# Blocks of expert slots in a two-layer decoder trunk: 14 for 16, with experts ranked by token count on chip

## Chip, cores, metric

One core of a Trainium2 chip. The metric is device time in microseconds (us) of one execution of the whole program: two layers, one launch.

## What is computed

Each of two layers has a mixer (attention over dilated windows and a convolution), a mixture of experts, and a gated input per layer. The change is in the mixture of experts. The reference, cut to that part (512 tokens, width 1024, 32 experts in 4 groups of 8, expert width 512, float32):

```python
gsel = argmax(h @ w_rg + b_rg)                 # one group per token
top_v, top_i = top_k(le[gsel], 2)              # two experts of that group, le = h @ w_re + b_re
gate = softmax(lg)[gsel] * softmax(top_v)
eid = gsel * 8 + top_i
...
hb = silu(xb @ w_gate[e]) * (xb @ w_up[e])     # xb: the tokens of expert e
out[tok] += gate * (hb @ w_down[e])
```

512 tokens choose two experts each, so 32 experts share 1024 rows. All 32 experts' weights are needed in each layer: 3 matrices of 2 MB each, as 12 tiles of 128x1024 float32 (512 KB) per expert, 384 tiles per layer.

## The kernel before

**Slots and blocks.** Every expert has `CAP` = 64 slots; a token's slot number is 64 times its expert plus its rank among that expert's tokens. Two experts make a block of 128 slots (a "pair", `p`), two blocks make a chunk `c`; a layer has 16 blocks in 8 chunks. An expert with more than 64 tokens is served by a loop (`overflow`, line 1213), whose number of rounds is computed on chip and read into registers.

**One chunk.** `onehots` builds, on VectorE, the 0/1 matrices that pick the chunk's 256 slots; `gather` turns them into the slots' activations (ps_xg, 64 matmuls of two terms, high and low); `gate_up` runs the gate and the up product of each block (ps_g, ps_u), with the 64 slots of an expert as the stationary operand and the weight tile streaming; the two experts of a block write the two halves of the same PSUM tile. `hidden` forms silu times up, `transp` turns it (ps_hT), `down` is the third product (ps_y), and `combine` adds the rows back to the tokens with the transposed 0/1 matrix (ps_c). The order on TensorE is written out in `moe`'s loop over `c`: gate and up of chunk c, down of chunk c-1, transposes of chunk c, gather for chunk c+1, combine of chunk c-1. After the combine of `c == OVC` (4) comes the loop for crowded experts; at `c` = 4 the table of the per-layer input is loaded (`load_embeddings`), and at 5 and 6 it is multiplied.

**Weights.** `pump` (line 234) issues the tiles from SP in the order of `self.items`: gate and up of two blocks, then down of the two before. A tile takes a buffer of pool `s4`, shared with everything else of the layer, and may be loaded as soon as a buffer is free; `KEEP` holds some back in each chunk. Before the expert stage, during the mixer, `RING` = 6, 18, 28 limits how many weight tiles may already be there at three points; another 8 half tiles (`late_items`, line 246) go to the other pool. All these loads go through SP's one queue, in program order: a load that waits for its buffer holds up all behind it. Each also waits for the landing of the one eight before.

**Routing.** For each of the four token tiles, `count` and `slots` find a token's experts and its slot (line 889 on); `route` then counts the tokens of each expert, and works out gates and the loop's rounds. The matmuls whose order is fixed are recorded through a wrapper class, so they all stand under line 94.

Of the kernel before, what the change touches and what calls it, by code (L numbers as in the profile page):

```python
# [26 lines left out]
CAP = 64  # L27
GS = 256
NPAIR = NE // 2
# [3 lines left out]
C_N1 = 592  # L33
# [23 lines left out]
RING = 6, 18, 28  # L57
KEEP = 6, 10, 6, 6, 8, 10, 12, 8
LAGS = 1, 2, 1, 5
OVC = 4  # L60
# [95 lines left out]
class Trunk:  # L156
    def __init__(self, ctx, tc, x, pT, wd, wg, wu, wdn, sm, gains, cst, out):
# [18 lines left out]
        self.items, self.item_tile, self.item_next, self.ring = [], {}, 0, 0  # L176
# [610 lines left out]
    def route_init(self):  # L787
# [3 lines left out]
        self.spos, self.base, self.slots = ([self.tn(4, f"{n}{i}") for i in range(2)] for n in ("sp", "sb", "sl"))  # L791
# [5 lines left out]
    def route_tile(self, t):  # L797
# [93 lines left out]
        pe.matmul(po, self.trib, mb(t), start=t == 0, stop=True)  # L891
        for i in range(2):
# [10 lines left out]

    def route(self):

        nc = self.nc
        v, act, pe = nc.vector, nc.scalar, nc.tensor
        for t in range(NT):
            pe.matmul(self.posb[:, 128:160], self.oneb, self.Mb[:, t * 32:(t + 1) * 32], start=t == 0, stop=t == NT - 1)
# [18 lines left out]
        cnt = self.posb[:, 128:160]  # L928
        v.tensor_scalar(cx, cnt, float(CAP), None, op0=OP.is_gt)
        for m in range(2, T // CAP):  # L930
            v.scalar_tensor_tensor(cx, cnt, float(m * CAP), cx, op0=OP.is_gt, op1=OP.add)
        self.ps.free()
# [32 lines left out]
    def moe(self, l):  # L965
# [85 lines left out]
        def down(p):  # L1051
            h_ = hT.pop(p)
            ps = [self.ps.get(F32, "y") for _ in range(2)]
            for f in range(4):
                for n in range(2):
                    for e in range(2):
                        pe.matmul(ps[n][64 * e:64 * e + 64], h_[:, f * P + e * CAP:f * P + (e + 1) * CAP],
                                  self.item_tile[l, "d", 2 * p + e, f][:, n * T:(n + 1) * T], start=f == 0, stop=f == 3)
                for e in range(2):
                    self.item_free((l, "d", 2 * p + e, f))  # L1060
                self.pump(keep=KEEP[self.c])
# [59 lines left out]
        NC2 = NPAIR // 2  # L1121
# [4 lines left out]
        self.s4.free()  # L1126
        for c in range(NC2):
# [34 lines left out]
            if c == OVC:  # L1162
                self.overflow(l)
# [320 lines left out]
```

## Time and profile before

| | us |
|---|---|
| median of 3 runs (lowest, highest) | 1884.03 (1882.94, 1884.06) |
| profiled execution, own time | 1876.28 |
| its span in the trace | 1874.5 |
| expert stage, first layer: first gate matmul to last down matmul | 397.2 to 880.6 |
| the same, second layer: SP resumes to last down matmul | 1325.5 to 1805.7 |

The profiled execution is 0.4% below the median; durations below are its own. The page names engines PE (matmul), PEld (weight load), DVE, ACT, POOL and SP; in rows of the page a name such as s_w<-wdn is a buffer of the program and the tensor that it was loaded from. wg, wu and wdn are the gate, up and down weights, raw tiles the dense weights of the mixer and the per-layer input, pT the per-layer input's table.

### The profile page before, as it was taken

The numbers are of one execution on the slowest core, as the hardware profiler recorded it, in microseconds if no ns is written. First come the engines' busy times: TensorE is split into PE (matmuls) and PEld (weight loads), VectorE is DVE, ScalarE is ACT, GpSimd is POOL, SyncE is SP. The second block draws the span as 40 slices with busy tenths as digits, with TensorE's granted clock in tenths as the row PEclk, the third lists the DMA queues.
The fourth block names the chain that finished last, engine by engine and source line by source line (L and its number), as shares of the span: only waits on it lengthen the run. The fifth ranks groups of instructions, "written<-read, shape, count | busy, mean of one in ns | idle before, by whom it ended". The sixth has DMA issues, their size and how long they took to land.

```text
span 1874.5 us, 23312 instructions
## 1 busy us (share of the span) xinstructions
PE 1790.9 (96%) x8532; PEld 1104.1 (59%) x8532; DVE 913.6 (49%) x2165; ACT 562.4 (30%) x1071; POOL 378.1 (20%) x201
## 2 busy tenths in 40 slices
PE   5999999999999989999989999999999999899987
PEld 4777777754555245454777767777545553455356
DVE  5587855463442243223657777536524432343146
ACT  4355443321111012113534445343211111021045
POOL 3445332401000001001444443242010000010021
PEclk9999999999999999999999999999999999999999
DMA  5212136389999899997231112554899999999951
GB/s 221 83 64 68 56 92 242 119 311 391 387 409 409 346 370 401 410 408 315 96 114 62 56 57 68 179 192 152 324 389 390 409 389 364 370 409 409 409 227 45
DMA packets 133319, 478.59 MB, mean 255 GB/s; under 512 B 14800, under 2 KB 15312, under 8 KB 133200
## 3 DMA queue, kind: packets, MB, share of 16 engines
q1 hardware_dynamic: 133200, 477.04, 66.9%
q8 instruction: 70, 1.15, 0.2%
q14 instruction: 49, 0.40, 0.1%
HBM read 474.89 MB, written 2.10 MB: 254 GB/s over the span
## 4 chain that ended last, share of the span: by engine, by line
PE 74%; DMA 10%; DVE 7%; issue 5%; ACT 2%; POOL 1%; SPq 0%; DVEq 0%; POOLq 0%; ACTq 0%
PE ps_g L94 11%; PE ps_u L94 10%; PE ps_y L94 9%; PE ps_z L290 5%; PE ps_z L289 5%; PE ps_z L291 5%; PE ps_xg L94 5%; PE ps_c L94 5%; DMA s_w<-wdn 4%; DMA s_w<-wg 3%; DMA s_w<-wu 2%; PE ps_tb L289 2%; PE ps_tb L290 2%; PE ps_tb L291 2%; PE ps_S L609 2%
## 5 line engine op out<-in xcount | busy, mean ns | idle before, releaser
L230 POOL TENSOR_TENSOR s_lo<-s_raw,s_hi 128x1024 fp32r<-128x1024 f32 x114 | 272.4, 2400 | 915.8 <-ACT s_hi L225 610.7
L94 PE MATMUL ps_g<-s_w,s_xg 128*64 128x512 f32 x1024 | 229.9, 602 | 11.2 <-DMA s_w<-wg 11.2
L94 PE MATMUL ps_y<-s_w,s_hT 128*64 128x512 f32 x1024 | 236.1, 595 | 3.5 <-DMA s_w<-wdn 2.9
L94 PE MATMUL ps_u<-s_w,s_xg 128*64 128x512 f32 x1024 | 231.2, 593 | 5.1 <-DMA s_w<-wu 4.9
L290 PE MATMUL ps_z<-s_hTl,s_hi 128*128 128x512 f32 x512 | 203.8, 398 | 0.0
L289 PE MATMUL ps_z<-s_hTh,s_hi 128*128 128x512 f32 x512 | 201.3, 393 | 0.0
L291 PE MATMUL ps_z<-s_hTh,s_lo 128*128 128x512 f32 x512 | 199.7, 390 | 0.0
L94 PEld LDWEIGHTS ps_y<-s_w,s_hT 128*64 128x64 f32 x1024 | 75.4, 137 | 159.9 <-issue 130.8
L94 PEld LDWEIGHTS ps_u<-s_w,s_xg 128*64 128x64 f32 x1024 | 74.0, 137 | 157.2 <-issue 141.1
L94 PEld LDWEIGHTS ps_g<-s_w,s_xg 128*64 128x64 f32 x1024 | 72.7, 139 | 155.4 <-issue 150.3
L501 DVE SCALAR_TENSOR_TENSOR s_acc<-ps_z,smt,s_acc 128x511 f32<-128x511 f32 (+27 forms) x210 | 153.8, 732 | 4.2
L1080 DVE TENSOR_TENSOR s_x<-s_x,ps_c 128x512 f32<-128x512 f32 x128 | 86.9, 688 | 89.4 <-PE ps_c L94 60.0
L225 ACT ACTIVATE s_hi<-s_raw 128x1024 fp32r<-128x1024 f32 x120 | 125.9, 1058 | 8.8 <-DMA s_raw<-wd 4.5
L94 PE MATMUL ps_xg<-s_OH,s_xh 128*128 128x256 f32 x476 | 117.4, 288 | 3.8 <-DVE s_OH L950 1.9
L1035 ACT ACTIVATE s_h<-ps_g,rs 128x512 f32<-128x512 f32 x32 | 22.0, 689 | 319.3 <-PE ps_g L94 286.5
L1046 ACT ACTIVATE s_hT<-ps_hT 128x512 f32<-128x512 f32 x32 | 17.7, 598 | 328.1 <-PE ps_hT L94 287.1
L94 PE MATMUL ps_xg<-s_OH,s_xl 128*128 128x256 f32 x476 | 115.9, 285 | 0.0
L290 PEld LDWEIGHTS ps_z<-s_hTl,s_hi 128*128 128x128 f32 x512 | 96.3, 188 | 21.2 <-issue 3.0
L289 PEld LDWEIGHTS ps_z<-s_hTh,s_hi 128*128 128x128 f32 x512 | 96.1, 188 | 21.3 <-issue 1.0
L1036 DVE SCALAR_TENSOR_TENSOR s_h<-s_h,ps_g 128x512 f32<-128x512 f32 x32 | 22.0, 688 | 177.5 <-ACT s_h L1035 177.5
L291 PEld LDWEIGHTS ps_z<-s_hTh,s_lo 128*128 128x128 f32 x512 | 96.3, 188 | 18.9
L94 PEld LDWEIGHTS ps_xg<-s_OH,s_xh 128*128 128x128 f32 x476 | 92.2, 194 | 5.7 <-issue 5.7
(256 smaller groups left out, 2852.4 us busy)
## 6 DMA issues: line engine op xcount, KB each, us to landing
s_w<-wu SPq DMA_DIRECT2D x256, 512.0 KB, 10.2
s_w<-wdn SPq DMA_DIRECT2D x256, 512.0 KB, 10.2
s_w<-wg SPq DMA_DIRECT2D x248, 512.0 KB, 10.2
s_raw<-wd SPq DMA_DIRECT2D x124, 512.0 KB, 3.5
s_w<-wg SPq DMA_DIRECT2D x16, 256.0 KB, 7.5
s_x<-x SPq DMA_DIRECT2D x4, 512.0 KB, 9.7
out<-s_n SPq DMA_DIRECT2D x8, 256.0 KB, 2.0
s_gain<-gains SPq DMA_DIRECT2D x3, 512.0 KB, 3.6
```

Of the source, the lines that this page charges most:

```text
L94: i = f(*a, **k)
L225: nc.scalar.activation(hi, raw, AF.Copy)
L230: nc.gpsimd.tensor_tensor(lo, raw, hi.bitcast(F32), op=OP.subtract)
L289: mm(out, lh, rh, start=start, stop=False)
L290: mm(out, lh, rl, start=False, stop=False)
L291: mm(out, ll, rh, start=False, stop=stop)
L501: v.scalar_tensor_tensor(o, i, w, o, op0=OP.mult, op1=OP.add)
L609: nc.tensor.matmul(ps[:, off:off + n], qk(0, i * P, (i + 1) * P)[r], qk(1, 0, n)[r], start=True, stop=True)
L1035: act.activation(t, pg, AF.Tanh, scale=rh[p])
L1036: v.scalar_tensor_tensor(t, t, 1.0, pg, op0=OP.add, op1=OP.mult)
L1046: act.activation(o, ps, AF.Copy)
L1080: v.tensor_add(xs, xs, ps)
```

## The change

The experts are no longer served in their own order, nor all with 64 slots. Experts 0 to 3 stay first, with 64 slots each (two blocks, "static"). The other 28 are ranked by token count on chip (`order_experts`): the eight smallest get 32 slots each, four to a block (blocks 2 and 3), the other 20 get 64 slots, two to a block. That makes 14 blocks, 7 chunks. The rank of every expert is turned into the list `oi`, and SP reads it into registers, from which the address of each tile of the ranked experts comes. A token's slot and the loop's condition follow the new bases: a small expert goes to the loop from its 33rd token on.

The weight order is now gate and up of blocks 0 and 1, down of blocks 0 and 1, gate and up of blocks 2 and 3, and then as before, one chunk apart. The order on TensorE is unchanged, except that the loop for crowded ones comes after the down products of the second chunk (`OVC` 1), ahead of its transposes. `RING` becomes 10, 21, 34 and `KEEP` is smaller. The core of the diff:

```diff
-NPAIR = NE // 2
+
+
+NST, NSM = 4, 8
+NDY = NE - NST
+BLK = ([(2 * i, 2 * i + 1) for i in range(NST // 2)]
+       + [tuple(range(NST + 4 * i, NST + 4 * i + 4)) for i in range(NSM // 4)]
+       + [(i, i + 1) for i in range(NST + NSM, NE, 2)])
+NB = len(BLK)
...
-RING = 6, 18, 28
-KEEP = 6, 10, 6, 6, 8, 10, 12, 8
+RING = 10, 21, 34
+KEEP = 2, 9, 5, 5, 5, 5, 2
 LAGS = 1, 2, 1, 5
-OVC = 4
+OVC = 1
...
         for l in range(self.L):
-            for c in range(NPAIR // 2 + 1):
-                for p in (2 * c, 2 * c + 1) if 2 * c < NPAIR else ():
-                    self.items += [(l, w, 2 * p + e, h) for w in ("g", "u") for h in range(4) for e in range(2)
-                                   if p or w == "u" or h < 4 - LATE]
-                for p in (2 * c - 2, 2 * c - 1) if c else ():
-                    self.items += [(l, "d", 2 * p + e, h) for h in range(4) for e in range(2)]
+            gu = [[(l, w, s, h) for w in ("g", "u") for h in range(4) for s in b
+                   if n or w == "u" or h < 4 - LATE] for n, b in enumerate(BLK)]
+            dn = [[(l, "d", s, h) for h in range(4) for s in b] for b in BLK]
+            seq = gu[:2] + dn[:2]
+            for c in range(1, NB // 2):
+                seq += gu[2 * c:2 * c + 2] + (dn[2 * c - 2:2 * c] if c > 1 else [])
+            self.items += sum(seq + dn[NB - 2:], [])
...
-            l, w, e, h = it = self.items[self.item_next]
+            l, w, s, h = it = self.items[self.item_next]
+            if s >= NST and (l > self.layer or self.order is None):
+                break
             if self.ring >= (limit if l <= self.layer else min(limit, PRE)):
                 break
             t = self.s4.get(F32, "w")
-            self.nc.sync.dma_start(t, self.dr[w][l, e, :, 1024 * h:1024 * (h + 1)])
+            self.nc.sync.dma_start(t, self.expert(w, l, s)[:, 1024 * h:1024 * (h + 1)])
             self.item_tile[it] = t
             self.item_next += 1
             self.ring += 1
+
+    def expert(self, w, l, s):
+
+        if s < NST:
+            return self.dr[w][l, s]
+        r = s - NST
+        if r not in self.order_v:
+            self.order_v[r] = self.nc.values_load(self.order[0:1, r:r + 1], engines=[mybir.EngineType.SP],
+                                                  min_val=0, max_val=NE - 1)
+        return self.dr[w][l, bass.ds(self.order_v[r], 1)].rearrange("o p f -> (o p) f")
...
+    def order_experts(self):
+
+        v = self.nc.vector
+        cnt = self.posb[:, 128:160]
+        key, rank, small, base, self.cnt, of, bs = (self.lgT[:, 32 * i:32 * i + 32] for i in range(7))
+        of, bs, ss = of[:, :NDY], bs[:, :8], bs[:, 8:16]
+        iota = self.cc(C_IOTA, 32)
+        tmp = self.s4.get(F32, "ord")
+        over = lambda a, n: a.unsqueeze(1).to_broadcast([P, n, 32])
+        down = lambda a, n: a.unsqueeze(2).to_broadcast([P, n, 32])
+        v.scalar_tensor_tensor(key, cnt, 32.0, self.cc(C_KEY, 32), op0=OP.mult, op1=OP.add)
+        t3 = tmp.rearrange("p (a b) -> p a b", b=32)
+        v.tensor_tensor(t3, over(key, 32), down(key, 32), op=OP.is_lt)
+        v.tensor_reduce(rank, t3, axis=AX.X, op=OP.add)
+        o3 = t3[:, :NDY]
+        v.tensor_tensor(o3, over(rank, NDY), down(iota[:, :NDY], NDY), op=OP.is_equal)
+        v.tensor_tensor(o3, o3, over(iota, NDY), op=OP.mult)
+        v.tensor_reduce(of, o3, axis=AX.X, op=OP.add)
+        oi = self.tn(NDY, "oi", I32)
+        v.tensor_copy(oi, of)
+        self.order, self.order_v = oi, {}
+
+        v.tensor_scalar(small, rank, float(NSM), 32.0, op0=OP.is_lt, op1=OP.mult)
+        v.scalar_tensor_tensor(base, rank, float(NSM - 1), small, op0=OP.subtract, op1=OP.mult)
+        v.scalar_tensor_tensor(base, rank, float(CAP), base, op0=OP.mult, op1=OP.subtract)
+        if CAP * NST != CAP // 2 * NSM:
+            v.tensor_scalar(base, base, float(CAP * NST - CAP // 2 * NSM), None, op0=OP.add)
+        v.tensor_copy(base[:, :NST], self.cc(C_BASE, NST))
+        v.tensor_add(self.cnt, cnt, small)
+        self.ps.free()
+        E8 = self.Ew[:, 0:256].rearrange("p (g e) -> p g e", e=32)
+        t8 = t3[:, :8]
+        for o, a in ((ss, small), (bs, base)):
+            v.tensor_tensor(t8, E8, over(a, 8), op=OP.mult)
+            v.tensor_reduce(o, t8, axis=AX.X, op=OP.add)
+        v.tensor_add(self.spos8, self.spos8, ss)
+        v.tensor_scalar(ss, self.spos8, float(CAP), 4096.0, op0=OP.is_ge, op1=OP.mult)
+        v.tensor_add(ss, ss, bs)
+        v.tensor_add(self.slots8, self.spos8, ss)
+        self.s4.free()
...
         def gate_up(p, xg, w, ps, hs):
+            m = P // len(BLK[p])
             for h in hs:
                 for k in range(2):
-                    for e in range(2):
-                        s = (2 * h + k) % 4 * GS + (2 * p % 4 + e) * CAP
-                        pe.matmul(ps[64 * e:64 * e + 64], xg[h // 2][:, s:s + CAP], self.half_item((l, w, 2 * p + e, h), k),
+                    for i, e in enumerate(BLK[p]):
+                        s = (2 * h + k) % 4 * GS + p % 2 * P + i * m
+                        pe.matmul(ps[m * i:m * i + m], xg[h // 2][:, s:s + m], self.half_item((l, w, e, h), k),
                                   start=h == 0 and k == 0, stop=h == 3 and k == 1)
-                for e in range(2):
-                    self.item_free((l, w, 2 * p + e, h))
+                for e in BLK[p]:
+                    self.item_free((l, w, e, h))
                 self.pump(keep=KEEP[self.c])
...
         for h in range(4):
             gather(oh, xg, h)
         self.s4.free()
+        with self.tc.issue_after(self.last_v):
+            self.order_experts()
         for c in range(NC2):
...
                 for p in prs:
                     down(p - 2)
+            if c == OVC:
+                self.overflow(l)
             for p, t in zip(prs, ts):
                 transp(p, t)
...
             if c:
                 combine((2 * c - 2, 2 * c - 1))
-            if c == OVC:
-                self.overflow(l)
             if c in (PEC, PEC + 1):
                 embeddings(c - PEC)
```

`down` takes the same step from two experts of 64 rows to `len(BLK[p])` experts of `m` rows; `NPAIR` becomes `NB` throughout; `route` takes its counts from `self.cnt`, to which 32 is added for a small expert.

Where the expert stage of the first layer begins, SP's queue (s_w are weight tiles, oi the list of ranks; in brackets what a row waits for: DMAHW an earlier transfer, PE and DVE those engines) before:

```order
L253 DMA s_w_3233<-wg 128x512 [waits DMAHW6_49,DVE_49]
L253 DMA s_w_3234<-wg 128x512 [waits DMAHW7_49]
L241 DMA s_w_3319<-wg 128x1024 [waits DMAHW0_49,PE_49]
L241 DMA s_w_3321<-wg 128x1024 [waits DMAHW1_49,PE_49]
L241 DMA s_w_3327<-wu 128x1024 [waits DMAHW2_49,PE_49]
L241 DMA s_w_3329<-wu 128x1024 [waits DMAHW3_49,PE_49]
```

and now:

```order
L274 DMA s_w_3234<-wg 128x512 [waits DMAHW6_49,DVE_49]
L274 DMA s_w_3235<-wg 128x512 [waits DMAHW7_49]
L263 TENSOR_LOAD oi [waits DVE_49]
L263 ISA x2
L263 TENSOR_LOAD oi
L263 ISA x2
...
L263 TENSOR_LOAD oi
L263 ISA x2
L252 DMA s_w_3326<-wdn 128x1024 [waits DMAHW0_49,PE_49]
L252 DMA s_w_3328<-wdn 128x1024 [waits DMAHW1_49,PE_49]
L252 DMA s_w_3342<-wdn 128x1024 [waits DMAHW2_49,PE_49]
```

Six register loads, the first of them waiting for DVE, have come between the eight late half tiles and the next weight tiles, which are now down tiles of the static experts.

What the first of these loads waits for is on DVE, in the new order (s_ord is the scratch tile that the comparisons use, s_lgT holds the small vectors):

```order
L943 TENSOR_TENSOR s_ord_3277<-s_lgT_2718 128x1024 [waits PE_49]
L944 TENSOR_REDUCE s_lgT_2718<-s_ord_3277 128x32 [waits DVE_49]
L946 TENSOR_TENSOR s_ord_3277<-s_lgT_2718,c_71 128x896 [waits DVE_49]
...
L947 TENSOR_TENSOR s_ord_3277<-s_ord_3277,c_71 128x896 [waits DVE_49]
...
L948 TENSOR_REDUCE s_lgT_2718<-s_ord_3277 128x28 [waits DVE_49]
...
L950 CAST oi<-s_lgT_2718 128x28 [waits DVE_49]
```

The comparison's scratch tile waits for PE: it takes the buffer of the first gather's 0/1 matrices. The next three operations on it each wait for the one before, and the list oi is cast at the end.

Around the loop for crowded experts SP had before (the second of its last branches carries waits for every engine and every DMA queue, in both kernels):

```order
L241 DMA s_w_5060<-wg 128x1024
L241 DMA s_w_5062<-wg 128x1024
L1219 COMPARE_AND_BRANCH
L1219 UNCONDITIONAL_BRANCH x2
...
L1219 REGISTER_ALU
L1219 COMPARE_AND_BRANCH
L1219 UNCONDITIONAL_BRANCH
L241 DMA s_w_5483<-wg 128x1024
L241 DMA s_w_5485<-wg 128x1024
L241 DMA s_w_5491<-wg 128x1024
L241 DMA s_w_5493<-wg 128x1024
```

and now:

```order
L252 DMA s_w_4123<-wg 128x1024
L1286 TENSOR_LOAD nov
L1286 ISA x2
L263 TENSOR_LOAD oi
L263 ISA x2
...
L1287 COMPARE_AND_BRANCH
L1287 UNCONDITIONAL_BRANCH
...
L263 ISA x2
L263 TENSOR_LOAD oi
L263 ISA x2
L252 ISA
L252 DMA s_w_4540<-wg 128x1024
```

The loop stood between two gate tiles late in the stage; it now stands after the first five gate tiles of block 5, and 15 register loads (of which the last is shown) stand between its end and the next weight tile. The address of each ranked tile takes one more operation on SP ("ISA").

## Rows read from the trace of the kernel before

**Rows 1.** Page, 40 slices of the span: PE busy tenths, then GB/s moved.

```profile
PE   5999999999999989999989999999999999899987
...
GB/s 221 83 64 68 56 92 242 119 311 391 387 409 409 346 370 401 410 408 315 96 114 62 56 57 68 179 192 152 324 389 390 409 389 364 370 409 409 409 227 45
```

**Rows 2.** Page, the chain that ended last: shares by engine.

```profile
PE 74%; DMA 10%; DVE 7%; issue 5%; ACT 2%; POOL 1%; SPq 0%; DVEq 0%; POOLq 0%; ACTq 0%
```

**Rows 3.** Page, groups: busy, mean ns of one | idle before, releaser.

```profile
L94 PE MATMUL ps_g<-s_w,s_xg 128*64 128x512 f32 x1024 | 229.9, 602 | 11.2 <-DMA s_w<-wg 11.2
```

**Rows 4.** Timeline of PE: start, duration, operation, count; 428 to 478 and 737 to 745.

```profile
428.78 0.36 PE L94 MATMUL ps_xg<-s_OH,s_xh 128*128 128x256 f32 x1
...
436.62 7.09 PE L94 MATMUL ps_g<-s_w,s_xg 128*64 128x512 f32 x32
443.54 7.04 PE L94 MATMUL ps_u<-s_w,s_xg 128*64 128x512 f32 x32
...
477.97 1.09 PE L94 MATMUL ps_hT<-c,s_h 128*128 128x128 f32 x8
...
737.47 0.40 PE L94 MATMUL ps_c<-s_yh,s_OHT 128*128 128x512 f32 x1
...
744.75 0.39 PE L94 MATMUL ps_pe<-s_hi,s_pTh 128*128 128x512 f32 x1
```

**Rows 5.** Timeline of SP in mid-stage: start and length of each run of issues.

```profile
578.49 9.27 SPq L241 DMA_DIRECT2D s_w<-wg  x8
588.70 9.29 SPq L241 DMA_DIRECT2D s_w<-wu  x8
```

**Rows 6.** Page, DMA issues: KB each, median us from issue to landing.

```profile
s_w<-wu SPq DMA_DIRECT2D x256, 512.0 KB, 10.2
```

**Rows 7.** Timeline of SP where the first layer's expert stage begins.

```profile
381.32 10.73 SPq L253 DMA_DIRECT2D s_w<-wg  x8
399.18 0.80 SPq L241 DMA_DIRECT2D s_w<-wg  x2
400.90 9.39 SPq L241 DMA_DIRECT2D s_w<-wu  x8
```

**Rows 8.** Busy time by window: PE, PEld, DVE, ACT, POOL; PE's granted clock, DMA share, GB/s.

```profile
402.00:414.00 12.00, 12.00 (x70) 5.32 (x68) 2.28 (x14) 2.11 (x5) 0.00 (x0) 1.00 0.91 314
600.00:640.00 40.00, 37.66 (x168) 16.16 (x168) 17.14 (x35) 3.52 (x6) 2.36 (x1) 1.00 0.86 336
680.00:688.00 8.00, 4.16 (x14) 1.30 (x16) 4.09 (x13) 0.00 (x0) 0.00 (x0) 0.79 0.57 200
684.00:686.00 2.00, 2.00 (x6) 0.60 (x8) 2.00 (x5) 0.00 (x0) 0.00 (x0) 0.50 0.55 127
```

**Rows 9.** Timelines of SP, then PE, at the end of the first layer's stage.

```profile
820.98 40.04 SPq L241 DMA_DIRECT2D s_w<-wdn  x32
861.99 9.27 SPq L207 DMA_DIRECT2D s_raw<-wd  x8
866.68 13.95 PE L94 MATMUL ps_y<-s_w,s_hT 128*64 128x512 f32 x64
```

**Rows 10.** Timeline of PE: the first gate group, behind the first gather.

```profile
397.22 7.09 PE L94 MATMUL ps_g<-s_w,s_xg 128*64 128x512 f32 x32
```

**Rows 11.** Page, a group of 512 elements on DVE; timeline of DVE at 411.

```profile
L1080 DVE TENSOR_TENSOR s_x<-s_x,ps_c 128x512 f32<-128x512 f32 x128 | 86.9, 688 | 89.4 <-PE ps_c L94 60.0
...
411.41 0.19 DVE L929 TENSOR_SCALAR cx<-ps_pos 128x32 f32<-128x32 f32 x1 [11.04 <-PE ps_pos L94]
```

**Rows 12.** Line 1218 on SP: count, duration in ns, min/median/max.

```profile
L1218 SPq TENSOR_LOAD <-nov x2: 287/386/484, 423.5 to 1350.9; - x2
L1218 SPq FUSED_REGOPS  x2: 159/168/178, 424.0 to 1351.2; - x2
```

**Rows 13.** Timelines of SP, then POOL, where the per-layer input is loaded.

```profile
609.14 0.33 SPq L1110 DMA_DIRECT2D s_pT<-pT  x1
622.82 0.80 SPq L207 DMA_DIRECT2D s_raw<-wd  x2
...
620.43 2.36 POOL L1112 TENSOR_TENSOR s_pTl<-s_pT,s_pTh 128x1024 fp32r<-128x1024 f32 x1 [153.60 <-ACT s_pTh L1111]
```

More of the change, by code (lines that the diff above doesn't have):

```diff
@@ L28 @@
 GS = 256
-NPAIR = NE // 2
+NST, NSM = 4, 8
[4 more added lines that the diff above has]
+NB = len(BLK)
 C_ID, C_ONE, C_BASE, C_PRIO, C_SLOT, C_IOTA = 0, 128, 256, 288, 320, 336
-C_N1 = 592
+C_KEY = 592
+C_N1 = 624
 C_BIAS, C_COS, C_SIN, C_TRI = (C_N1 + 512 * i for i in range(4))
@@ L174, in __init__ @@
         self.queues, self.adv_n = [], 0
-        self.items, self.item_tile, self.item_next, self.ring = [], {}, 0, 0
+        self.items, self.item_tile, self.item_next, self.ring, self.order = [], {}, 0, 0, None
         for l in range(self.L):
-            for c in range(NPAIR // 2 + 1):
-                for p in (2 * c, 2 * c + 1) if 2 * c < NPAIR else ():
-                    self.items += [(l, w, 2 * p + e, h) for w in ("g", "u") for h in range(4) for e in range(2)
-                                   if p or w == "u" or h < 4 - LATE]
-                for p in (2 * c - 2, 2 * c - 1) if c else ():
-                    self.items += [(l, "d", 2 * p + e, h) for h in range(4) for e in range(2)]
+            gu = [[(l, w, s, h) for w in ("g", "u") for h in range(4) for s in b
[5 more added lines that the diff above has]
+            self.items += sum(seq + dn[NB - 2:], [])
     def tn(self, cols, name, dt=F32, bufs=1):
@@ L790, in route_init @@
         self.Mb = self.tn(128, "Mb", BF)
-        self.spos, self.base, self.slots = ([self.tn(4, f"{n}{i}") for i in range(2)] for n in ("sp", "sb", "sl"))
+        self.spos8, self.base8, self.slots8 = (self.tn(2 * NT, n) for n in ("sp", "sb", "sl"))
+        self.spos, self.base, self.slots = ([a[:, i * NT:(i + 1) * NT] for i in range(2)]
+                                            for a in (self.spos8, self.base8, self.slots8))
+        self.order = None
         self.rc = self.tn(4, "rc")
@@ L891, in route_tile @@
         pe.matmul(po, self.trib, mb(t), start=t == 0, stop=True)
+        if t == NT - 1:
+            for s in range(NT):
+                pe.matmul(self.posb[:, 128:160], self.oneb, mb(s), start=s == 0, stop=s == t)
         for i in range(2):
@@ L904, in route @@
     def route(self):
         nc = self.nc
-        v, act, pe = nc.vector, nc.scalar, nc.tensor
-        for t in range(NT):
-            pe.matmul(self.posb[:, 128:160], self.oneb, self.Mb[:, t * 32:(t + 1) * 32], start=t == 0, stop=t == NT - 1)
+        v, act = nc.vector, nc.scalar
         w = self.lgw.rearrange("p (t e) -> p t e", t=NT)
@@ L927, in route @@
         cx, cum, tmp = self.tn(32, "cx"), self.tn(32, "cum"), self.tn(32, "cumt")
[L928 to L932, printed above, removed]
+        v.tensor_scalar(cx, self.cnt, float(CAP), None, op0=OP.is_gt)
+        for m in range(2, T // CAP + 1):
+            v.scalar_tensor_tensor(cx, self.cnt, float(m * CAP), cx, op0=OP.is_gt, op1=OP.add)
         src = cx
@@ L1053, in down @@
             ps = [self.ps.get(F32, "y") for _ in range(2)]
+            m = P // len(BLK[p])
             for f in range(4):
                 for n in range(2):
[L1056 to L1060, printed above, removed]
+                    for i, e in enumerate(BLK[p]):
+                        pe.matmul(ps[n][m * i:m * i + m], h_[:, f * P + i * m:f * P + i * m + m],
+                                  self.item_tile[l, "d", e, f][:, n * T:(n + 1) * T], start=f == 0, stop=f == 3)
+                for e in BLK[p]:
+                    self.item_free((l, "d", e, f))
                 self.pump(keep=KEEP[self.c])
@@ L1117, in load_embeddings @@
             self.pp = []
-        NC2 = NPAIR // 2
+        NC2 = NB // 2
         xg = [self.s4.get(F32, "xg") for _ in range(2)]
@@ L1167, in moe @@
         self.load_chunks(self.lim)
-        down(NPAIR - 2)
-        down(NPAIR - 1)
+        down(NB - 2)
+        down(NB - 1)
         self.nc = nc
@@ L1201, in then @@
                 first(t - 1)
-        combine((NPAIR - 2, NPAIR - 1), then)
+        combine((NB - 2, NB - 1), then)
         first(NT - 1)
@@ L1414, in constants @@
     c[:, C_PRIO:C_PRIO + 32] = 32 - np.arange(32)
+    c[:, C_KEY:C_KEY + 32] = np.arange(32) + 1e6 * (np.arange(32) < NST)
     c[:, C_SLOT:C_SLOT + 16] = i[:, None] + P * np.arange(16)
```

## Prediction

> **What bounds the kernel now.** I read the page's slices first. PE is busy 96% of the span, and yet in the two stretches of the expert stage the DMA row stands at 9 and the GB/s row at 370 to 411 [rows 1]. The chain of waits puts 74% on PE and only 10% on DMA [rows 2], and the group of the gate matmuls shows 11.2 us of waiting on weights in both layers [rows 3]. That looks like a kernel bound by PE. The timeline of one stage corrects it. A chunk of two blocks costs PE four gate and up groups of 443.54 - 436.62 = 6.92 us, 13.95 us of down [rows 9], some 0.8 of the transposes' 1.09, a gather of 436.62 - 428.78 = 7.8 us and a combine of 744.75 - 737.47 = 7.3 us: about 57.4 us [rows 4]. The same chunk needs four experts of 12 tiles of 512 KB. SP issues eight of them per 588.70 - 578.49 = 10.21 us, each waiting for the landing of the one eight before, 10.2 us after its issue [rows 5, 6]: 1.28 us a tile, 410 GB/s, so 48 tiles take 61.4 us. **The stage is bound by the DMA queue, with PE only 4 us a chunk shorter.** PE's waits are small because it always trails the stream a little. So I price the change in lost time of the DMA stream, and take PE's work only as a check.
>
> On the stream before, in the first layer: SP stops at 381.32 + 10.73 = 392.1 with the ring full, resumes at 399.18 and flows from 400.90 [rows 7]. In 402 to 414 it waits for slots: 314 of 410 GB/s, 12 x 96/410 = 2.8 us lost. Around the loop for crowded experts, 680 to 688, 200 GB/s: 8 x 210/410 = 4.1 us lost. In 600 to 640, 336 GB/s: 40 x 74/410 = 7.2 us lost [rows 8]. The last down tile is issued at 820.98 + 40.04 = 861.0 and lands at about 871.2, while the last down matmul ends at 866.68 + 13.95 = 880.6 [rows 9]: PE trails by 9.4 us.
>
> **The change part by part** (one layer, in stream time; a plus is slower).
>
> *Two blocks fewer.* If four 32-slot experts run side by side in the time in which two 64-slot ones run now, eight small experts cost PE two blocks where they cost four: a chunk, 57.4 us, goes. If they don't, only its gather, combine and transposes go, 7.8 + 7.3 + 1.1 = 16.2 us. On the stream it is 0 either way: the weights stay 384 tiles a layer, 491 us at 1.28. What hides it is that stream. It pays only at the end: PE no longer trails by 9.4 us but by the work of the last tiles, which I put at a tenth of the down row, 1.5 us. **-7.9**, bounds -9.4 and 0.
>
> The rows show two experts side by side and never four: one gate instruction lasts 602 ns [rows 3], and yet 32 of them follow each other in 6.92 us, 0.22 each [rows 4]. The Trainium skill (TensorEngine Tiling (Array Packing), Theoretical Speedup) gives up to 4x for a dimension of 32, and the same page (Key Properties) says that changing the tiling mode drains TensorE. The first half favours the change and the second speaks against it, but by either the stream's sum stays as it is.
>
> *Ring of 34 tiles for 28.* Six more tiles arrive before the stage, in a stretch where PE bounds: 6 x 1.28 = **-7.7**, bounds -7.7 and 0 (should the mixer pay for the earlier burst of ten tiles instead of six, I keep 0 to +4 for it in the range).
>
> *The slot wait in 402 to 414* goes, since 18 slots are free when the first gate group starts: **-2.8**, bounds -2.8 and 0.
>
> *The new wait ahead of the first tile.* On SP, six register loads of the ranks stand ahead of ten static down tiles, and the first waits for the DVE. Its chain starts only when the first gather has released its slot, at 397.22 [rows 10]. It holds two operations of 1024 elements and three of 896. The trace has none so large; the nearest, 512 elements, takes 0.688 us [rows 11]. Doubling bounds it at 1.38, and I take 1.25 and 1.1; with some six small ones at 0.2 that is about 7 us, so the ranks are there at 404.2. A register load on SP took 287 to 484 ns and the operation behind it 159 to 178 ns [rows 12]: 0.55 us the pair, six are 3.3. The first tile starts at 407.5 for 399.18: **+8.3**, bounds +5 (small loads, chain at 5.5) and +10. Behind that wait stand all later tiles; PE does not feel it at first, with 34 tiles in hand. On DVE the chain fills the 11.04 us idle gap that ends at 411.41 [rows 11].
>
> *The loop moves from after the fifth chunk's combine to after the second chunk's down blocks.* It still runs zero times: counting the reference's routing, the eight smallest of experts 4 to 31 have at most 26 tokens, no expert over 55, in both layers. But its branch waits for all engines and all DMAs, and behind it SP now has 15 more register loads before its first tile: 15 x 0.55 = 8.3 us. With about 2 us of drain and exit and 2 of first landing, the stream is empty for 12 us instead of 4.1: **+7.9**, bounds +4 and +16. What is late next: only four slots are free then; the next waits for the gather and four more for the combine, 16.2 us of PE work after the exit, about the time that SP needs for the loads and four tiles (8.3 + 5.1).
>
> [...]
>
> *The table of the per-layer input* is loaded at an earlier chunk. Today the load at 609.14 is followed by nothing until 622.82: the next load takes its slot, which POOL frees only at 620.43 + 2.36 [rows 13]. In the new order two tiles go first and the wait stands behind them: 2 x 1.28 = **-2.6** of the 7.2, bounds -7.2 and 0.
>
> *The tail.* The eight chunks behind the last down tile are issued from 861.99 [rows 9], and landed as PE finished. With PE no longer late, they end some 9 us after it, beside its last combine of 7.3 us and the transposes: **+3**, bounds 0 and +8. The four count matmuls ahead of the first gather: +0.2.
>
> Sum: -7.9 - 7.7 - 2.8 + 8.3 + 7.9 - 2.6 + 3 + 0.2 = -1.6 a layer, **-3 us for both**. The profiled execution took 1876.28 us, 0.4% under the median of 1884.03; the sum makes it 1873, and the median **1881 us**. A measurement of this kernel can tell about 0.2% (3.8 us) from no change, so this is about even.
>
> **The rivals.**
> *Cheap waits (faster).* The loads pipeline and cost 0.2 us each, the first wait is +6, the loop is +2.7, the tail +1: 6 - 7.7 - 2.8 + 2.7 - 2.6 - 7.9 + 1.2 = -11.1 a layer, 1862 us. For it: the loads behind the first wait for nothing, and the trace has none back to back. Against: each that it has took 287 ns or more, with its next operation behind it.
> *The restart after the loop (slower).* The clock was granted at 0.50 in 684 to 686, after 680 to 684 had left PE idle [rows 8]; at the lower of its two levels, 1.2 GHz, the 16.2 us of transposes, gather and combine start slowly, and they now gate the slots. Everything that PE loses there beyond the 13.4 us of SP's own restart, plus the queue's depth, is lost by the stream. A gap of 20 us for 12, about half of the 16.2 lost again, gives +8, -1.6 + 8 = +6.4 a layer, 13 for both, 1897 us; it decides where PE takes more than some 17 us from the loop's exit to its next gate group.
> *Four are not side by side.* PE needs 41 us more a layer than I think; it then trails again at the end by some 5: +3.4 a layer, 1888 us.
> *It doesn't do what it says:* the loop iterates. One round loads an expert's 12 tiles with everything stopped, 15 us and more: +30 and up, 1911 us. The counts speak against it.
>
> **How the numbers follow.** About even 0.42 (its own range 1871 to 1891), cheap waits 0.27, restart 0.22, no concurrency 0.06, iterating loop 0.03. The even case lies below 1880.2 with two fifths of its chance, within 0.2% with about as much: faster 0.17 + 0.27, same 0.17 and a little from the others, slower the rest: 0.42, 0.20, 0.38. The range takes the first rival's centre and 5 us beyond, and the second's and 10 us: 1857 to 1907.
>
> **What would show it.** In the new profile the DMA should stand empty from about 394 to 408, then hold 409 GB/s; a second hole of about 12 us near 527 to 540 should hold 15 register loads on SP; small blocks should show 0.11 us per gate instruction; and the last down tile should land under 2 us before the last down matmul ends. PE busy should fall by about 115 us with the span nearly as it was. I am wrong if the stream's rate differs from 1.28 us a tile, if either hole is more than 5 us off, or if the mixer grows.

## The result: 1917 us, and the profile after

The changed kernel took 1917.26 us (median of 4 runs, 1915.16 to 1917.73) against 1883.49 (4 runs): ratio 1.0178, 95% interval 1.0161 to 1.0196. It is slower by 34 us, where about even was forecast, and outside the range of 1857 to 1907. Its profiled execution took 1917.1 us, span 1915.3; the one before had 1874.5, so the two traces lie 40.8 us apart, 7 us more than the medians.

The page of the changed kernel, first engines, then slices of PE and GB/s, then the three groups of expert matmuls (busy, mean ns of one, idle before and its releaser), to be set beside [rows 1, 3]:

```profile
PE 1786.3 (93%) x8324; PEld 1066.2 (56%) x8324; DVE 882.1 (46%) x2115; ACT 546.8 (29%) x1039; POOL 378.3 (20%) x201
...
PE   5999998989879999999989999989997999999997
...
GB/s 218 87 56 67 65 138 184 113 254 419 419 250 419 419 357 418 419 419 276 91 119 57 64 58 67 208 176 117 271 419 418 271 419 419 365 419 419 419 163 44
...
L102 PE MATMUL ps_u<-s_w,s_xg 128*64 128x512 f32 (+1 forms) x1024 | 249.7, 596 | 13.8 <-DMA s_w<-wu 13.4
L102 PE MATMUL ps_y<-s_w,s_hT 128*64 128x512 f32 (+1 forms) x1024 | 238.1, 598 | 10.4 <-DMA s_w<-wdn 9.5
L102 PE MATMUL ps_g<-s_w,s_xg 128*64 128x512 f32 (+1 forms) x1024 | 224.7, 595 | 5.3 <-DMA s_w<-wg 5.1
```

PE is busy for 93% of the span, and in both stages the GB/s row has a slice, at 250 and at 271, that was not there. The three groups' idle times come to 29.5 us for 19.8 before. But PE's busy time counts a matmul that crawls behind its weights as busy: it fell by 4.6 us only, from 1790.9 us, where the forecast had 115. So the loss has to be looked for in the timelines.

I cut both traces at the same places. First gate group to last down matmul: 483.4 us before and 496.1 after in the first layer, 482.1 and 491.8 in the second. From the first layer's last down matmul to the second's first gate group, the stretch with the next mixer: 443.0 and 451.3. Both parts are longer, by 10 to 13 and by 8.

**The mixer.** Timeline of SP, after (start, length, count of issues), from the first burst of weight tiles to the first tile of the stage:

```profile
273.33 2.82 SPq L252 DMA_DIRECT2D s_w<-wg  x4
276.25 6.50 SPq L252 DMA_DIRECT2D s_w<-wu  x7
283.66 0.33 SPq L216 DMA_DIRECT2D s_raw<-wd  x1
...
388.89 11.02 SPq L274 DMA_DIRECT2D s_w<-wg  x8
415.83 7.84 SPq L252 DMA_DIRECT2D s_w<-wdn  x10
```

The same burst before:

```profile
273.05 2.82 SPq L241 DMA_DIRECT2D s_w<-wg  x4
275.97 2.80 SPq L241 DMA_DIRECT2D s_w<-wu  x3
278.86 0.69 SPq L207 DMA_DIRECT2D s_raw<-wd  x1
```

And what PE waited for in 270 to 345, after (total, times, longest), then before:

```profile
PE ps_yb L310 <- ACT s_hi L234: 3.8, 1, 3.8
PE ps_yb L312 <- POOL s_lo L239: 2.7, 2, 1.7
PE ps_wo L311 <- POOL s_lo L239: 0.6, 1, 0.6
```

```profile
PE ps_yb L291 <- POOL s_lo L230: 1.6, 2, 1.0
```

Eleven weight tiles stand in front of the mixer's next own load (s_raw) instead of seven; it starts at 283.66 for 278.86, and PE waits 7.1 us for split weights instead of 1.6.

**The stage's start.** The DVE chain for the ranks, its first and its last operation:

```profile
405.90 1.23 DVE L943 TENSOR_TENSOR s_ord<-s_lgT 128x1024 f32<-128x1024 f32 x1 [0.45 <-PE ps_xg L102]
...
411.93 0.17 DVE L950 CAST oi<-s_lgT 128x28 int32<-128x28 f32 x1
```

and the register loads on SP (count, ns min/median/max):

```profile
L263 SPq TENSOR_LOAD <-oi x56: 262/265/470, 412.1 to 1495.2; - x56
L263 SPq FUSED_REGOPS  x56: 147/147/174, 412.7 to 1495.5; - x56
```

The first gate group starts at 405.8 and the list is there at 412.1. Six register loads later, 0.27 + 0.15 us each and 0.56 us from one to the next, SP issues the first tile at 415.83: 10 us behind the gather, where 10.3 was forecast (407.5 less 397.2).

**The second chunk and the loop.** Timeline of PE, then windows (the last three columns: granted clock, DMA share, GB/s):

```profile
445.06 6.95 PE L102 MATMUL ps_g<-s_w,s_xg 128*32 128x512 f32 x52
...
515.78 13.96 PE L102 MATMUL ps_y<-s_w,s_hT 128*64 128x512 f32 x64
541.59 1.97 PE L102 MATMUL ps_hT<-c,s_h 128*128 128x128 f32 x8 [11.85 <-SPq L263]
...
560.10 7.09 PE L102 MATMUL ps_g<-s_w,s_xg 128*64 128x512 f32 x32
```

```profile
445.00:516.00 71.00, 62.97 (x260) 12.08 (x260) 4.79 (x12) 2.21 (x4) 9.27 (x4) 1.00 1.03 419
520.00:580.00 60.00, 48.15 (x244) 26.79 (x242) 19.71 (x45) 7.99 (x15) 0.00 (x0) 0.89 0.75 284
534.00:568.00 34.00, 26.41 (x142) 19.75 (x144) 12.73 (x32) 5.25 (x11) 0.00 (x0) 0.81 0.55 181
536.00:538.00 2.00, 0.00 (x0) 0.00 (x0) 0.00 (x0) 0.00 (x0) 0.00 (x0) 0.50 0.86 350
542.00:544.00 2.00, 2.00 (x12) 2.00 (x11) 1.09 (x5) 1.00 (x2) 0.00 (x0) 0.50 0.03 8
546.00:548.00 2.00, 2.00 (x14) 2.00 (x14) 1.13 (x4) 0.84 (x2) 0.00 (x0) 0.70 0.00 0
700.00:715.00 15.00, 14.47 (x66) 4.58 (x62) 5.54 (x11) 2.32 (x3) 2.38 (x1) 1.00 0.65 241
```

The four-expert group ends 52 of its instructions, 0.6 us each, within 6.95 us, one per 0.13 where the two-expert groups have one per 0.22 [rows 4]; in the trace four start within 0.02 us of each other, and the next four 0.43 us later. Four run side by side. But the second chunk then runs at the stream's pace: 445 to 516 at 419 GB/s, 71 us for 4 x 6.9 = 27.6 us of work. At the loop PE stands for 11.85 us while the last transfers land. Its clock is granted at 0.50 (the lower level, 1.2 GHz) from 536 to 538, when it stands idle, to 542 to 544, and at 0.70 on the mean of 546 to 548. Its transposes take 1.97 us for 1.09 [rows 4], and from the loop's exit to the next gate group it needs 560.1 - 541.6 = 18.5 us. Over 534 to 568 the stream moves 181 of 419 GB/s: 34 x 238/419 = 19.3 us lost, for 4.1 before [rows 8]. In the second layer it is 17.0 us (317 GB/s over 1460 to 1530).

**The table and the tail.** SP around the table's load, then SP and PE at the stage's end:

```profile
697.42 0.34 SPq L1176 DMA_DIRECT2D s_pT<-pT  x1
698.67 1.53 SPq L216 DMA_DIRECT2D s_raw<-wd  x2
710.94 4.15 SPq L252 DMA_DIRECT2D s_w<-wu  x7
```

```profile
836.24 39.15 SPq L252 DMA_DIRECT2D s_w<-wdn  x32
876.25 9.06 SPq L216 DMA_DIRECT2D s_raw<-wd  x8
882.42 0.39 PE L102 MATMUL ps_pe<-s_hi,s_pTh 128*128 128x512 f32 x1
...
887.96 13.95 PE L102 MATMUL ps_y<-s_w,s_hT 128*64 128x512 f32 x64
```

The two raw tiles now go first, but behind them SP still stands, from 700.2 to 710.94, 10.7 us for 13.4 before: 15 x 178/419 = 6.4 us of the stream by the window of 700 to 715. At the end PE's last down group ends at 901.9, 26.5 us behind the last issue, where it was 19.6 [rows 9]. Just before that group stands a product of the per-layer input (ps_pe, 882.4 to 888.0). It still belongs to chunks 5 and 6, counted from 0; of eight chunks that left one behind it, of seven chunk 6 is the last.

### The profile page after: what moved, and what is told of

Read it like the earlier page. It is cut to its first block, busy times and chain, and to the rows that moved or that the text cites. A ratio compares the mean times of both kernels' runs of the same rounds, so it can differ in the third digit from the quotient of the medians.

```text
span 1915.3 us, 24331 instructions
## 1 busy us (share of the span) xinstructions
PE 1786.3 (93%) x8324; PEld 1066.2 (56%) x8324; DVE 882.1 (46%) x2115; ACT 546.8 (29%) x1039; POOL 378.3 (20%) x201
## 5 line engine op out<-in xcount | busy, mean ns | idle before, releaser
L102 PE MATMUL ps_u<-s_w,s_xg 128*64 128x512 f32 (+1 forms) x1024 | 249.7, 596 | 13.8 <-DMA s_w<-wu 13.4
L102 PE MATMUL ps_y<-s_w,s_hT 128*64 128x512 f32 (+1 forms) x1024 | 238.1, 598 | 10.4 <-DMA s_w<-wdn 9.5
L102 PE MATMUL ps_g<-s_w,s_xg 128*64 128x512 f32 (+1 forms) x1024 | 224.7, 595 | 5.3 <-DMA s_w<-wg 5.1
L102 PEld LDWEIGHTS ps_u<-s_w,s_xg 128*64 128x64 f32 (+1 forms) x1024 | 68.7, 130 | 188.5 <-issue 115.0
L102 PEld LDWEIGHTS ps_y<-s_w,s_hT 128*64 128x64 f32 (+1 forms) x1024 | 69.5, 129 | 175.4 <-issue 106.7
L102 PEld LDWEIGHTS ps_g<-s_w,s_xg 128*64 128x64 f32 (+1 forms) x1024 | 64.9, 130 | 152.7 <-issue 114.1
L1146 DVE TENSOR_TENSOR s_x<-s_x,ps_c 128x512 f32<-128x512 f32 x112 | 75.4, 685 | 82.8 <-PE ps_c L102 60.9
L102 PE MATMUL ps_xg<-s_OH,s_xh 128*128 128x256 f32 x412 | 107.1, 298 | 3.7 <-DVE s_OH L1014 3.7
L102 PE MATMUL ps_xg<-s_OH,s_xl 128*128 128x256 f32 x412 | 105.4, 294 | 0.0
L1102 DVE TENSOR_TENSOR s_h<-s_h,ps_u 128x512 f32<-128x512 f32 x28 | 19.2, 687 | 166.6 <-PE ps_u L102 166.6
```

The source lines that it names most:

```text
L102: i = f(*a, **k)
L1102: v.tensor_mul(t, t, pu)
L1146: v.tensor_add(xs, xs, ps)
```

## Experiments

The theory after the result (A): the burst delays the mixer and brings nothing; the loop's new place makes it a halt of PE and stream together; the register loads add to both holes; and PE's two blocks less fall where PE waits for weights. The rivals are named in each expectation. All times are medians; before was 1883.4 to 1883.9 us in every comparison.

**Old ring limits.** `RING = 6, 18, 28` in the changed kernel.

> The changed kernel with the old ring limits (6, 18, 28 weight tiles for 10, 21, 34). Theory A (the early burst of weight tiles holds up the mixer's own loads): the first gather ends near 397 us again instead of 405, 8 us earlier in each layer; but six fewer tiles, 7.5 us of stream a layer, are there when the expert stage begins. If the stage is bound by the stream, the two cancel and the time stays at 1917 us, give or take 4. Rival B (the mixer's delay counts in full, since PE and not the stream sets the end of the stage): about 16 us less, 1901. Rival C (the larger ring has nothing to do with the mixer's delay): the first gather stays at 405 and the time rises to about 1930.

1899.9 us, ratio to before 1.0089 (1.0060 to 1.0119): 17 us less, as rival B said, but not for its reason. Counting SP's issues ahead of the late half tiles gives 34 whole tiles in this kernel, in the changed one and in the kernel before: the last fill before the stage has no limit but free buffers. So nothing is lost with the old limits, and the run does not tell whether PE or the stream sets the end.

**Only the first limit.** `RING = 6, 21, 34`.

> The changed kernel with only the first ring limit put back (6, 21, 34). Theory A: it is the burst at the first limit, eleven weight tiles ahead of the mixer's next own load, that delays the mixer; without it the first gather ends near 397 us in the first layer, and most of the six extra tiles still arrive before the stage: up to 8 us less a layer, 1901 to 1907 us. Rival (the total of 34 delays the mixer, by the buffers it holds): the first gather stays at 405, 1917 us.

1901.4 us, 1.0100 (1.0083 to 1.0117): all of the effect is in the first number. From the first layer's last down matmul to the second's first gate group it takes 446.2 us, 5 less than after.

**The limits alone on the kernel before.** `RING = 10, 21, 34`, nothing else.

> The kernel before with only the ring limits of the change (10, 21, 34). Theory A: 34 whole tiles stand ahead of the eight late half tiles with either set of limits, since the last fill before the stage has no limit; so nothing is gained, and the burst at the first limit delays the mixer by 5 to 6 us a layer: 1894 to 1896 us. The forecast's view (six more tiles in hand): 15 us less for the stream, 1868 to 1875. Its rate of the stream (409 or 419 GB/s) also shows whether the higher rate in the traces of the changed kernel belongs to the chip or to the kernel.

1900.3 us, 1.0087 (1.0070 to 1.0103): slower by 16.4 us, more than I expected, 8.2 a layer. That is half of the whole loss, from a line that has nothing to do with blocks.

**Register loads late**, each behind the last weight transfer before its first use.

```diff
-            self.nc.sync.dma_start(t, self.expert(w, l, s)[:, 1024 * h:1024 * (h + 1)])
+            self.last_w = self.nc.sync.dma_start(t, self.expert(w, l, s)[:, 1024 * h:1024 * (h + 1)]).ins
...
-            self.order_v[r] = self.nc.values_load(self.order[0:1, r:r + 1], engines=[mybir.EngineType.SP],
-                                                  min_val=0, max_val=NE - 1)
+            with self.tc.issue_after(self.last_w) if self.last_w else nullcontext():
+                self.order_v[r] = self.nc.values_load(self.order[0:1, r:r + 1], engines=[mybir.EngineType.SP],
+                                                      min_val=0, max_val=NE - 1)
```

> The changed kernel with each register load of a rank held on SP behind the weight transfer before its first use, so that ten static tiles go ahead of the first wait for the ranks, and no row of 15 loads stands behind the loop. Theory A: the empty stretch of the stream at the stage's start shrinks by about 10 us (the tiles start near 405.5 instead of 415.8) and the one at the loop by about 7 us (15 loads of 0.45 us), 17 us a layer for a stage bound by the stream; as PE trails the stream by 17 us at the end, part of that is not seen: 1885 to 1900 us. Rival B (the loop's drain and PE's work behind it set the restart, not SP's loads, and PE sets the end): under 10 us less in all, 1908 to 1917.

1909.4 us, 1.0138 (1.0120 to 1.0157): 8 us less. The first tile goes out at 408.4, 2 us behind the first gate group's start instead of 10, and yet the stages are only 7 and 4 us shorter. That is rival B's size, and at the loop its reason too: the stream's hole there stays, with 293 GB/s for 284 in 520 to 580, 18.0 us for 19.3, and 16.9 for 17.0 in the second layer. So the fifteen loads behind the loop do not set its restart.

```profile
520.00:580.00 60.00, 48.98 (x252) 26.50 (x250) 20.41 (x46) 8.65 (x16) 0.00 (x0) 0.91 0.77 293
```

**No loop.** The call of `overflow` is left out.

> The changed kernel without the loop for crowded experts, which runs no round on these inputs (left out: the rounds that an expert with too many tokens would need). This is the whole price of the loop at its new place. Theory A: the 19 us hole in the stream at 534 to 567 us goes, 15 to 19 us a layer less for the stream, 30 to 38 us in all if PE follows: 1880 to 1890 us. Rival B (PE's own work after it sets the end): 12 us a layer, the time that PE stood idle before the transposes, 1893. Rival D (the loop costs what it cost before, 4 us a layer): 1909.

1891.6 us, 1.0045 (1.0028 to 1.0062): 25.7 us less, 12.9 a layer: rival B's number, PE's stand of 11.85 us and one more. But it is also what the stream gets back. It still loses something at this place, 3.0 and 4.3 us in the two layers by the same windows, so 16.3 and 12.7 us of its hole have gone.

```profile
520.00:580.00 60.00, 60.00 (x332) 28.74 (x332) 20.82 (x46) 8.03 (x16) 0.00 (x0) 1.00 1.00 398
```

From the transposes to the next gate group PE takes 16.0 us here (531.8 to 547.8, clock 1.00), for 18.5 behind the loop.

**The loop behind the combine**, same chunk.

```diff
-            if c == OVC:
-                self.overflow(l)
             for p, t in zip(prs, ts):
                 transp(p, t)
...
                 combine((2 * c - 2, 2 * c - 1))
+            if c == OVC:
+                self.overflow(l)
```

> The changed kernel with the loop for crowded experts in the same chunk (the second), but after its transposes, gather and combine, where it stood relative to them before the change. Theory A: the loop is dear at its new place because PE's 16 us of transposes, gather and combine stand behind it instead of beside the drain of the stream; moved, PE does them while the last transfers land, the empty stretch of the stream falls from 19 us to about 10 and PE's stand from 11.9 to 2 or so: 8 to 10 us less a layer, 1897 to 1901. Rival B (any halt of all queues in this chunk, with the full ring ahead of it, costs the same): 1915 to 1919.

1907.9 us, 1.0125 (1.0109 to 1.0142): 9.3 us less, between the two forecasts. PE's wait at the loop and the stream around it:

```profile
PE ps_g L102 <- DVEq L1287: 2.3, 1, 2.3
...
530.00:570.00 40.00, 37.74 (x200) 21.46 (x198) 19.45 (x43) 7.33 (x15) 0.00 (x0) 0.96 0.74 288
```

The wait is 2.3 us for 11.85, 9.5 less; the stream's loss is 40 x 131/419 = 12.5 us for 19.3, and 12.7 for 17.0 in the second layer, 5.5 less on the mean. The time fell by 4.7 a layer. So the place matters, and the time follows the stream's loss, not PE's stand.

**The loop early in the kernel before**, second chunk, ahead of the transposes.

> The kernel before, 16 blocks, with only the loop moved to the change's place: second chunk, after the down products, ahead of transposes, gather and combine. Theory A: the halt costs PE the drain of eight transfers, about 8 to 10 us instead of 5.6, and then the slots for the stream wait for the gather and combine: 5 to 12 us a layer, 1894 to 1908 us. Rival (the place is as good as the old one, and only the register loads behind it are dear): 1882 to 1886.

1897.6 us, 1.0072 (1.0053 to 1.0090): 13.7 us slower, 7 a layer, as A said. PE's wait there:

```profile
PE ps_hT L94 <- DMA s_w<-wg: 11.3, 1, 11.3
```

and at the old place, in the timeline of before:

```profile
683.84 6.45 PE L94 MATMUL ps_g<-s_w,s_xg 128*64 128x512 f32 x22 [5.57 <-DMA s_w<-wg]
```

11.3 us for 5.57, without any loads of ranks behind the loop. So the place alone is dear.

**Small blocks' gate and up twice**, into a tile that nobody reads: the direct test of what PE's saving is worth.

```diff
+            junk = self.ps.get(F32, "j") if len(BLK[p]) == 4 else None
...
+                    for i, e in enumerate(BLK[p]) if junk is not None else ():
+                        s = (2 * h + k) % 4 * GS + p % 2 * P + i * m
+                        pe.matmul(junk[m * i:m * i + m], xg[h // 2][:, s:s + m], self.half_item((l, w, e, h), k),
+                                  start=True, stop=True)
...
+            if junk is not None:
+                self.ps.free()
```

> The changed kernel with every gate and up product of the two small blocks computed a second time into a PSUM tile that nothing reads: 27.6 us more of PE's work a layer, 55 us in all, half of what the two blocks less had saved. Theory A: PE's saving falls where it waits for the stream (the second chunk takes 71 us for 27.6 us of work), so the time barely moves: 1917 to 1925 us. Rival B (PE's work sets the time): 1945 to 1972.

1914.1 us, 1.0162 (1.0145 to 1.0179): not slower than the changed kernel at all. The added matmuls are in the trace, and the second chunk, with them, takes the same 71 us:

```profile
L102 PE MATMUL ps_j<-s_w,s_xg x512: 592/592/617, 448.8 to 1461.0; 128*32 128x512 f32 x171
```

```profile
448.00:519.00 71.00, 67.97 (x511) 17.94 (x512) 4.79 (x12) 2.21 (x4) 9.04 (x4) 1.00 1.03 419
```

Half of PE's saving can be spent again at no cost in this kernel: it lay where PE waits for 64 tiles of weights.

**Three repairs together**: first limit 6, late loads, loop behind the combine.

> The changed kernel with three repairs together: first ring limit 6 again, each register load behind the transfer before its first use, the loop after the combine of the second chunk. Singly the first took 16 us off, the second 8; if theory A holds for the third (16 to 20) and they overlap little, 1917 - 16 - 8 - 16 = 1877 us, faster than the kernel before by 0.3%. Rival B (they repair the same hole twice; PE's tail sets the end): 1885 to 1893, no faster than before.

1884.5 us, 1.0000 (0.9990 to 1.0009): level with before, at the edge of rival B's range, but not for its reason. The three repairs gave 15.9, 7.9 and 9.3 us singly, 33.1 in all, and together give 32.8: they do not repair the same hole. A had put the third at 16. With its dear parts mended, a kernel with some 57 us less of PE's work a layer (the prediction's chunk) is no faster.

**The table's hole in the kernel before.** The table goes to two tiles of the other pool, `s2`, so no weight tile waits for its slot.

```diff
-            praw = self.s4.get(F32, "pT")
-            nc.sync.dma_start(praw, self.dr["pT"][l])
-            act.activation(self.pT[0].t[0], praw, AF.Copy)
-            nc.gpsimd.tensor_tensor(self.pT[1].t[0], praw, self.pT[0].t[0].bitcast(F32), op=OP.subtract)
-            self.s4.free()
+            praw = [self.s2.get(F32, "pT") for _ in range(2)]
+            for k, r in enumerate(praw):
+                a = slice(T * k, T * k + T)
+                nc.sync.dma_start(r, self.dr["pT"][l, :, a])
+                act.activation(self.pT[0].t[0][:, a], r, AF.Copy)
+                nc.gpsimd.tensor_tensor(self.pT[1].t[0][:, a], r, self.pT[0].t[0][:, a].bitcast(F32), op=OP.subtract)
+            self.s2.free(2)
```

> The kernel before with only the table of the per-layer input loaded into two tiles of the other pool, so that the next load doesn't wait for its slot. Theory A: the 7.2 us hole of the stream at 609 to 623 us goes; PE lost 5.5 us to it in 620 to 680, so 4 to 6 us less a layer, 1872 to 1876 us. Rival (the ring bridges it, and PE's tail sets the end): 1882 to 1886.

1866.1 us, 0.9912 (0.9895 to 0.9928): faster than both kernels, by more than I expected. From the first gate group to SP's last down issue it now takes 456.7 and 456.1 us in the two layers, for 463.8 and 463.4: the hole of 7.2 us [rows 8] counts in full. SP no longer stands after the table's load, and 600 to 640 runs at 408 GB/s with PE busy throughout, for 336 and 37.66 us [rows 8]:

```profile
611.50 1.57 SPq L1112 DMA_DIRECT2D s_pT<-pT  x2
614.07 1.62 SPq L207 DMA_DIRECT2D s_raw<-wd  x2
616.63 8.08 SPq L241 DMA_DIRECT2D s_w<-wu  x8
```

```profile
600.00:640.00 40.00, 40.00 (x197) 18.93 (x197) 18.96 (x43) 4.48 (x9) 2.51 (x2) 1.00 1.03 408
```

**The same repair in the combination.**

> The combination of three repairs (first ring limit 6, register loads late, loop after the combine) with only the per-layer input's table moved to the other pool, its product left in the sixth and seventh chunk. Set beside the kernel before with the same table repair (1866 us), it says what 14 blocks for 16 are worth once no other part of the change is in the way. Theory A (PE's saving falls where PE waits for the stream, and the halt and the late start of the stream still cost): 1868 to 1878 us, not faster than 1866. Rival B (the table's hole was all that hid the saving): 1845 to 1860, faster than the kernel before with the table repair.

1872.9 us, 0.9948 (0.9931 to 0.9964), in A's range: faster than before, but 7 us slower than the 16 blocks with the same repair. Its last down issue comes 454.1 and 453.9 us after the first gate group, 2 to 3 us sooner than there; but its last down group ends 25.5 and 23.9 us behind that issue, for 18.4 and 18.6.

**The product of the per-layer input moved as well**, to the third and fourth chunk (`PEC = 2`, first `KEEP` 5).

> The combination of three repairs (first ring limit 6, register loads late, loop after the combine) with two more: the per-layer input's product moved from the sixth and seventh chunk to the third and fourth, where PE waits for weights, and its table loaded into two tiles of the other pool, so that no weight tile waits for its slot. Theory A: what PE saved in the small blocks is only worth something if work from its bound tail moves there; 11 us of PE's tail a layer and the 7 us hole of the stream go: 1855 to 1870 us, faster than the kernel before by about 1%. Rival (the stream sets the time after all, and the moved loads only shift the hole): 1878 to 1885.

1874.7 us, 0.9950 (0.9934 to 0.9967), a miss: no faster than the run above, which leaves the product where it was. SP and PE at the first stage's end, in the run above and then here:

```profile
812.20 39.61 SPq L253 DMA_DIRECT2D s_w<-wdn  x32
863.32 13.95 PE L103 MATMUL ps_y<-s_w,s_hT 128*64 128x512 f32 x64
```

```profile
823.25 39.60 SPq L253 DMA_DIRECT2D s_w<-wdn  x32
865.75 13.95 PE L103 MATMUL ps_y<-s_w,s_hT 128*64 128x512 f32 x64
```

The end did get shorter: 879.7 - 862.85 = 16.9 us behind the last issue for 877.3 - 851.8 = 25.5, and 18.4 for 23.9 in the second layer. But the last issue comes later, 462.6 and 463.9 us after the first gate group for 454.1 and 453.9. The stream lost what PE gained; which of the moved loads or held-back tiles does it was not tried.

**Other pairs of experts** in the kernel before: e with e + 16.

> The kernel before with experts e and e + 16 in a block instead of 2e and 2e + 1 (slots and weights follow; rounds of the loop, of which there are none on these inputs, would take the wrong weights and are left out of account). All traces of the changed kernel show the stream at 419 GB/s, all of the kernel before at 409. Theory A: the rate hangs on which two experts' tiles alternate in the stream (neighbours in memory before, distant ones after the ranking): 419 GB/s here too, 8 to 10 us of stream a layer less, and where PE trails the stream half of that shows: 1865 to 1880 us. Rival (the rate comes with the addresses from registers, not with the experts): 409 GB/s, 1884.

1888.3 us, 1.0026 (1.0016 to 1.0036), its stream at 409 GB/s. So which experts alternate, at least in this pairing, does not make the 419 GB/s that every kernel with ranks shows; whether the addresses from registers do was not tried.

## Why the prediction was wrong

The sum had -1.6 us a layer; the medians say +17. By its steps:

- *"Ring of 34 tiles for 28: -7.7"* failed at its premise. 34 whole tiles stand ahead of the late halves in either kernel, which the order of SP's queue would have shown; the gain is 0. The mixer's side, kept at "0 to +4", is 8.2 a layer by the run of the limits alone. This step is off by some 16 us, the largest error.
- *"Two blocks fewer: 0 on the stream, -7.9 at the end."* The first half is right, and the doubled gate and up show it. The second is wrong by 15 us: PE does not catch up with the last tile but trails the last issue by 26.5 and 26.1 us, for 19.6 and 18.7. Behind the last up group it still owes the down groups of two chunks, a combine and, now that there are seven chunks, a product of the per-layer input. Every run with 14 blocks and this order trails by 23.9 to 26.5 us, every one with 16 by 18.1 to 19.8; with the product moved ahead it was 16.9 and 18.4.
- *"The loop moves: +7.9, bounds +4 and +16."* The stream's hole grew by 15.2 in the first layer, near the upper bound; in time the loop costs 12.9 a layer where it now stands. The rival named for it, the restart, had the mechanism, the size (a gap of 20 us) and the mark: PE needed 18.5 us from the exit to the next gate group, over the 17 from which it was to decide, with the clock at 0.50. The fifteen loads, which the sum priced there, hardly change the hole.
- *"The table: -2.6"* came as -0.8: SP stood 10.7 us behind it all the same, and the hole is 6.4 us for 7.2. I took it for a small term of both kernels; closed in the kernel before, it is worth 17 us in all, the largest gain over the kernel before that these runs show.
- *"The new wait ahead of the first tile: +8.3"* was right in size (10 us behind the gather against 10.3), and so was its 0.55 us a load: from one to the next it is 0.56. No run shows the 0.2 us of the rival of cheap waits. Of the 33 us that this wait and the fifteen loads hold SP in both layers, the time gave back 8 when they went.
- *The stream's rate*, 1.28 us a tile, was taken as given. It was 1.25 (419 GB/s), which the prediction named as a sign of being wrong. An estimate from the two rates: 346 tiles still to come at 0.03 us are some 10 us a layer in the change's favour, by luck, since its cause is open. It hides part of the other errors.
- The slot wait is gone, four experts run side by side, and the loop runs no rounds, as forecast.

Accounting in time of the stream held. Outside its holes the stream runs at 419 GB/s, and what a hole costs shows in the time: the table's in the kernel before, and at the loop what of the hole the runs took away. The stretches of the two traces add up, a layer on the mean of both: 4.1 us from the first gate group to the last issue (holes larger by some 14, less 10 for the rate; the sum had 10.8 for the holes), 7.1 from there to the last down matmul, 8.4 in the mixer, 0.8 at the end, 20.4 in all. The profile before lies 7 us under its median, which makes it 20.4 for the medians' 17. What the accounting lacked is that a hole closed in one place can stay open for another reason (late loads, the halt without its wait), and that the end and the mixer are not the stream's. The three single repairs add up to the 33 us that they give together, all but 1 of the loss.

## What to carry to other kernels

Before counting a prefetch limit as a gain, count the transfers that stand ahead of the stage in the queue's order: another limit may bind, and what moves forward may only push other loads back. Work saved on an engine that waits for its weights in that stretch is worth nothing; ask where the saved time falls, chunk by chunk, and test it by doing the work twice. When the number of steps changes, look at what then falls into the last one. A load that takes a slot which the very next load needs back holds a whole queue: a small buffer elsewhere took 17 us off here.

## What the runs showed of the hardware that was not expected

- The stream ran at 419 GB/s in every kernel with ranked experts and at 409 in every one without (issue to landing 9.9 and 10.2 us), also where both ran on one chip, one after the other. Pairs of distant experts alone stayed at 409; the cause is open.
- A register load on SP took 0.265 us at the median with 0.147 for the operation behind it, back to back, less than the 0.386 and 0.168 of the two single ones before [rows 12]; but from one load to the next it is 0.56 us.
- PE's granted clock fell to 0.50 while it stood idle at the loop (0.50 in 536 to 538), and was still 0.50 in 542 to 544 and 0.70 in 546 to 548, with PE busy again from 541.59.
